# An encoder trunk on one Trainium2 core: another order of casts and sums at the begin of the MLP products

## The chip, the cores and the metric

The kernel runs on one core of a Trainium2 chip. The metric is device time in microseconds (us) of one execution; lower is better. Its engines are called as the profile calls them: PE (TensorE, matrix products; PEld is its weight load), DVE (VectorE), ACT (ScalarE), POOL (GpSimd) and SP (SyncE, which here issues most transfers; its own queue is SPq).

## What is computed

A trunk of two layers over 1024 frames with 1024 channels. Layer 0 mixes with RWKV-7 and gated DeltaNet heads, layer 1 with chunked softmax attention. Each layer then has the MLP on which the change works:

```python
for i in range(DEPTH):                      # DEPTH = 2
    h = rmsnorm(x, norm_mix_g[i])
    ...                                     # even: rwkv7_group and gdn_group, odd: chunk_band_attention
    x = x + mix                             # mix = heads @ w_out
    hf = rmsnorm(x, norm_ffn_g[i])
    x = x + jnp.square(jax.nn.relu(hf @ mlp_w1[i])) @ mlp_w2[i]
    x = x + rmsnorm(p[i] @ ple_w_proj[i], ple_norm_g[i]) * jax.nn.sigmoid(x @ ple_w_gate[i])
```

`mlp_w1` is 1024x4096 and `mlp_w2` 4096x1024; all is float32.

## The kernel before, in words

**Split products.** A float32 product is made of three matmuls on fp32r operands: each operand is cast to a high half (`hi`, on ACT), and the rest is its low half (`lo`, a subtraction on DVE). `mm3` multiplies hi by hi, hi by lo and lo by hi. So every operand that PE takes costs one pass of ACT and, behind it, one of DVE. `split` does both; `split_start` is the cast alone and `split_end` the subtraction alone.

**The MLP by sub-products.** Activations are held as channels by frames (128 partitions x 1024 frames), and a pair of channel tiles by two frame halves makes four blocks, `b11`, `b12` (even tile, first and second half of the frames), `b21`, `b22` (odd tile). The first product runs over 16 pairs p of hidden tiles; each pair needs seven sub-products instead of eight, in the order m = 1, 2, 5, 6, 7, 3, 4, each of 12 matmuls of 128x512. Their operands are blocks or differences of blocks: on the activations' side `cmb[m][j]` for four pairs j of channel tiles, on the weights' side what `prepare(p, m)` makes from `w1`. In the traces and the program's order the activations' operands are `r` (m = 1, 2, 7, 3), `xw`, `x` (5, 6) and `act` (4), and the weights' are `act` (the first `w`). A step, or slot, is k = 7p + q.

**Begin of the MLP.** `Trunk.tail` first makes eight output tiles n of the out-projection on the second half of the frames, 24 matmuls each; the first half came earlier. For each n: `load_x` brings the residual tile into `xr[n % 2]`; `first_half(n)` scales its first half by the norm's weight into `xs` (L1284) and, for odd n, casts `cmb[1]` and `cmb[2]` of the pair from it; then the projection; `ev_out(n)` evacuates it onto the residual (L1312), stores it, scales the second half, and for odd n below 7 makes `cmb[3]`, 5, 6, 7 and 4 (subtractions L1306, casts L1264, low halves L1268); `square` (L1289 and on) puts squares on ACT and sums them on POOL into `acc`. The norm's row factor is applied after the product. So the MLP can begin before it is known; `row_stats` sums `acc` over partitions by matmuls with `ones` (PE) behind slot 3, takes the mean on DVE (`ms`) and the inverse root on POOL, and `to_rows` turns it into rows `rs` behind slot 6 by transposes on PE (`ident`). POOL then scales hidden blocks by `rs`.

**What sets the order.** Up to and with the eight output tiles a scheduler places instructions by a time model, inside the limits of the data. From the line `self.pinned = True` on, each engine takes its instructions in the order in which the code emits them. The fourth pair's operands (n = 6 and 7) of products 5, 3, 6, 7 and 4 and the first pair's weights are made there, between the first seven products, by the list `ahead`: one entry per slot q of p = 0, carried out ahead of that slot's product.

**Handover to the second product.** It has 56 steps of 24 matmuls. Ahead of its first steps (p = 15), `load_hidden` splits hidden tiles that come back from memory, `load_block` fetches blocks of `w2`, `w_split` casts them and `w_sum` (POOL) adds or subtracts blocks. Blocks and splits are issued at slots q = 3, 5 and 4, 6 of p = 15.

Of the kernel before, what the change touches and what calls it, by code (L numbers as in the profile page):

```python
# [17 lines left out]
P = 128  # L18
# [97 lines left out]
class Trunk:  # L116
# [239 lines left out]
    def row_stats(self, accs, out, scale=1.0 / D, eps=1e-6, pool=False):  # L356

        nc = self.nc
        nt = out.shape[-1]
        ps = self.stat_bank()  # L360
        for i in range(nt):
            self.mm(ps[:, i:i + 1], accs[i // 4][:, (i % 4) * P:(i % 4 + 1) * P], self.ones[:, 0:1],
                             start=True, stop=True)
        ms = self.sm.tile([P, NT], F32, tag="ms", name="ms")[:, 0:nt]
# [829 lines left out]
    def tail(self, i, xsrc):  # L1194
# [13 lines left out]
        with ExitStack() as es:  # L1208
# [48 lines left out]
            sq = sq_pool.tile([P, HB], F32, tag="sq", name="sq")  # L1257
# [29 lines left out]
            def square(n, hf):  # L1287
# [4 lines left out]
                else:  # L1292
                    A.activation(sq, t, AF.Square)
                    G.tensor_tensor(accs[hf], accs[hf], sq, op=ALU.add)

            def first_half(n):
                scaled(n, 0)
                if n % 2:
                    j = n // 2
                    split(cmb[1][j], b11)  # L1300
                    split(cmb[2][j], b21)
                square(n, 0)

            def combine(m, j):
                u, v, w = {5: (b12, b12, b11), 6: (b22, b22, b12), 7: (b11, b22, b11), 4: (b21, b21, b22)}[m]
                V.tensor_tensor(u, v, w, op=ALU.subtract)  # L1306
                split(cmb[m][j], u)

            def ev_out(n):
                def f(ps):  # L1310
# [120 lines left out]
            def w_sum(g, m, n):  # L1431
# [4 lines left out]
                G.tensor_tensor(o, u, v, op=op)  # L1436

            def w_split(g, m, n):
# [28 lines left out]
            def ev_1(p, q, m, ps):  # L1467
                o = held[p]
                d = 8 if p == 0 else 7 * p + 2
# [36 lines left out]
            for p in range(16):  # L1506
# [6 lines left out]
                for q, m in enumerate(order):  # L1513
# [637 lines left out]
```

## Time and profile before

| | us |
|---|---|
| median of three runs | 3146.58 (3139.86 to 3149.94) |
| profiled execution | 3152.89 |
| its span, first to last instruction | 3151.1 |
| PE busy | 3020.8 (96%) |
| DVE busy | 2218.4 (70%) |
| ACT busy | 1410.3 (45%) |
| POOL busy | 1248.0 (40%) |
| mean granted clock of PE | 0.966 |

The profile is of one execution, 1.8 us longer than its span. A busy share over the whole span says little of a single place: PE can be full on average and wait in one stage. A timeline row gives the start and the busy time in us, the engine, the line of the kernel, the operation, out<-in, the shapes, how many instructions it holds (x), and in brackets the idle time of the engine just ahead of it with what ended it. A row of a stretch gives its length, the busy time and number of instructions of the engines named, then the granted clock of PE, the busy share of the DMA engines and GB/s. Layer 0's MLP begins at about 1016 us and hands over to its second product near 1350; layer 1's at about 2410 and 2750.

### The profile page before, as it was taken

To read this page: it belongs to the slowest core of one execution; us is meant where nothing else is said; L and a number is where in the kernel's file an instruction comes from. 1 tells how busy PE (TensorE), PEld (TensorE's weight loads), DVE (VectorE), ACT (ScalarE), POOL (GpSimd) and SP (SyncE) were. 2 spreads that over 40 slices of the span, in tenths; PEclk is the share of its full clock that TensorE was granted. 3 is DMA by queue.
4 is the path that set the end of the run, shared out by engine and by line. 5 is a ranking of instruction groups with operands and counts; after the bars stand their busy time and mean duration, and the time that the engine had idled before them with its cause. 6 is when DMAs were issued, how large, how long until landed. Compare 5 with 4: busy or idle time off the path is not lost.

```text
span 3151.1 us, 45431 instructions
## 1 busy us (share of the span) xinstructions
PE 3020.8 (96%) x17096; PEld 2525.7 (80%) x17096; DVE 2218.4 (70%) x3666; ACT 1410.3 (45%) x2464; POOL 1248.0 (40%) x1404
## 2 busy tenths in 40 slices
PE   7999999999998999999999999999998999999999
PEld 5887778788786788878888899998876888778887
DVE  6555774566847788878676587887867888777672
ACT  4343443343525454444334365665645454543341
POOL 6344342343612565557263200000113565656442
PEclk8999898999899999999999999999999999999999
DMA  3311112112234244574423211110154344664323
GB/s 115 102 60 60 44 32 77 60 60 83 103 126 144 100 151 149 179 257 168 143 87 132 95 36 43 41 49 27 65 181 167 117 147 151 221 220 168 133 89 105
DMA packets 160700, 353.60 MB, mean 112 GB/s; under 512 B 42592, under 2 KB 42720, under 8 KB 160480
## 3 DMA queue, kind: packets, MB, share of 16 engines
q1 hardware_dynamic: 128224, 291.97, 27.8%
q10 hardware_dynamic: 32256, 58.73, 4.9%
q8 instruction: 134, 2.20, 0.3%
q14 instruction: 86, 0.70, 0.1%
HBM read 251.02 MB, written 99.61 MB: 111 GB/s over the span
## 4 chain that ended last, share of the span: by engine, by line
PE 44%; DVE 6%; ACT 2%; issue 2%; DMA 1%; POOL 1%; SPq 0%; ACTq 0%; DVEq 0%; POOLq 0%
PE dps L173 40%; PE sc L173 2%; PE pt L178 1%; PE po L173 1%; DVE pb L2000 1%; POOL late L113 0%; DVE ptile L340 0%; PE dps L178 0%; DVE act L113 0%; DVE gw L1667 0%; ACT F L1942 0%; ACT pb L2004 0%; DVE r L1268 0%; DMA wraw<-in_w_out 0%; POOL act L113 0%
## 5 line engine op out<-in xcount | busy, mean ns | idle before, releaser
L173 PE MATMUL dps<-r,act 128*128 128x512 f32 x4440 | 1044.1, 394 | 21.5 <-ACT act L113 13.2
L173 PEld LDWEIGHTS dps<-r,act 128*128 128x128 f32 x4440 | 837.3, 189 | 214.1 <-ACT act L113 15.1
L173 PE MATMUL dps<-xg,whi 128*128 128x512 f32 x1280 | 439.1, 419 | 13.2 <-ACT xg L342 6.9
L113 ACT CAST act<-late 128x512 fp32r<-128x512 f32 (+1 forms) x282 | 200.8, 729 | 390.3 <-DVE late L113 213.6
L113 DVE TENSOR_TENSOR act<-late,act 128x512 fp32r<-128x512 f32 (+1 forms) x282 | 339.3, 1211 | 37.0 <-ACT act L113 31.0
L173 PE MATMUL dps<-wq,act 128*128 128x384 f32 x1536 | 305.4, 346 | 5.8 <-DVE vs L1909 2.1
L173 PEld LDWEIGHTS dps<-xg,whi 128*128 128x128 f32 x1280 | 248.3, 199 | 69.2 <-ACT xg L342 6.9
L173 PEld LDWEIGHTS dps<-wq,act 128*128 128x128 f32 x1536 | 266.1, 191 | 10.1 <-DVE vs L1909 3.3
L173 PE MATMUL dps<-xg,wlo 128*128 128x512 f32 x640 | 266.6, 417 | 2.1 <-DVE wlo L299 2.1
L113 POOL TENSOR_TENSOR late<-late 128x512 f32<-128x512 f32 (+1 forms) x104 | 179.9, 1733 | 106.8 <-ACT late L113 73.3
L113 POOL TENSOR_TENSOR late<-late,rs 128x512 f32<-128x512 f32 x88 | 133.9, 1528 | 86.3 <-DVE late L113 69.4
L1916 POOL TENSOR_TENSOR sq<-qk 128x512 f32<-128x512 f32 x32 | 34.7, 1083 | 311.4 <-ACT qk L1904 294.4
L113 DVE TENSOR_TENSOR r<-act,r 128x1024 fp32r<-128x1024 f32 (+1 forms) x80 | 148.4, 1859 | 5.5 <-ACT r L113 5.5
L173 PEld LDWEIGHTS dps<-xg,wlo 128*128 128x128 f32 x640 | 126.6, 198 | 29.1 <-DVE wlo L299 3.4
L173 PE MATMUL dps<-xw,act 128*128 128x512 f32 x576 | 139.2, 393 | 1.5 <-ACT act L113 1.5
L113 DVE TENSOR_TENSOR late<-late,dps 128x512 f32<-128x512 f32 x154 | 105.2, 683 | 44.6 <-PE dps L173 41.4
L298 ACT CAST whi<-wraw 128x1024 fp32r<-128x1024 f32 x78 | 81.6, 1046 | 119.2 <-PE dps L173 94.8
L173 PEld LDWEIGHTS dps<-xw,act 128*128 128x128 f32 x576 | 107.5, 188 | 28.2 <-ACT act L113 3.1
L2004 ACT ACTIVATE pb<-pb,mx 128x640 f32<-128x640 f32 (+4 forms) x128 | 89.6, 700 | 83.1 <-DVE mx L2002 79.5
L113 DVE TENSOR_TENSOR late<-late 128x512 f32<-128x512 f32 x120 | 123.8, 1032 | 1.0
L299 DVE TENSOR_TENSOR wlo<-wraw,whi 128x1024 fp32r<-128x1024 f32 x78 | 99.0, 1271 | 34.1 <-ACT whi L298 33.0
L113 ACT ACTIVATE late<-late 128x512 f32<-128x512 f32 x176 | 110.9, 631 | 25.7 <-POOL late L113 22.9
(490 smaller groups left out, 5865.7 us busy)
## 6 DMA issues: line engine op xcount, KB each, us to landing
late<-in_w SPq DMA_DIRECT2D x100, 512.0 KB
hc<-late ACTq DMA_DIRECT2D x154, 256.0 KB
act<-hc SPq DMA_DIRECT2D x76, 512.0 KB
wraw<-in_w_in SPq DMA_DIRECT2D x56, 512.0 KB
hraw<-hc SPq DMA_DIRECT2D x36, 512.0 KB
hc<-sums ACTq DMA_DIRECT2D x70, 256.0 KB
act<-in_w SPq DMA_DIRECT2D x28, 512.0 KB
wraw<-in_w_out SPq DMA_DIRECT2D x21, 512.0 KB
```

What stands on the lines that cost most here:

```text
L113: return lambda *args, **kw: self.tc.keep_in_program_order(f(*args, **kw))
L173: r = self.nc.tensor.matmul(out, lhsT, rhs, start=start, stop=stop)
L178: return self.nc.tensor.transpose(out, in_, ident)
L298: nc.scalar.copy(hi, raw)
L299: nc.vector.tensor_tensor(lo, raw, hi.bitcast(F32), op=ALU.subtract)
L1916: G.tensor_tensor(sq, q4[:, 8 * e:8 * e + 8], q4[:, 8 * e:8 * e + 8], op=ALU.mult)
L2000: V.tensor_tensor_reduce(S, ps[:, 0:n * P], toep[:, (5 - n) * P:], op0=ALU.add, op1=ALU.max, scale=1.0, scalar=NEG, accum_out=mx[:, 0:1])
L2004: A.activation(S, S, AF.Exp, bias=mx[:, 1:2], accum_out=l)
```

## The change

The change has seven parts, all in `tail` and the two functions that it calls for statistics.

- `row_stats` becomes `row_sums` (the matmuls with `ones`) and `row_norms` (mean and inverse root). At the MLP's begin the sums come behind slot 4 (was 3), the norms behind slot 5, `to_rows` behind slot 7 (was 6); the first pair's scaling moves from slot 8 to 9.
- `first_half(n)` casts `cmb[1]` or `cmb[2]` for every n, directly from the residual with the norm's weight as the scale (L1309 in the numbering after: scalar_tensor_tensor on DVE), where before both were cast for odd n from `xs`. It still fills `xs`.
- Two tiles `sq` in turn hold the squares, where there was one.
- `ev_out(n)` for odd n below 7 starts the operands of 5 and 3 together and then ends them; the square of tile 7's second half moves into the pinned part.
- `ahead` is written anew: sums and casts of the activations' operands (`x5`, `x3`, ...) and of the first pair's weights (`w2`, `w5`, ...) begin together and end later, in turn.
- `w_sum` of the first block row, m = 5, runs on VectorE instead of GpSimd.
- At p = 15 one hidden tile is split and one block fetched at each of q = 1 to 4, where two of each were at q = 3 and 5; the weight splits come at q = 3 and 5 instead of 4 and 6.

```diff
+        self.row_norms(self.row_sums(accs, out), out, scale, eps, pool)
...
-            sq = sq_pool.tile([P, HB], F32, tag="sq", name="sq")
+            sqs = ring([sq_pool.tile([P, HB], F32, tag=f"sq{q}", name="sq") for q in range(2)])
...
             def first_half(n):
+                c, t, g = cmb[1 + n % 2][n // 2], xr[n % 2][:, hs[0]], self.vec("ffng", 8 * i + n)
+                A.activation(c[:, 0], t, AF.Copy, scale=g)
+                V.scalar_tensor_tensor(c[:, 1], t, g, c[:, 0].bitcast(F32), op0=ALU.mult, op1=ALU.subtract)
                 scaled(n, 0)
-                if n % 2:
-                    j = n // 2
-                    split(cmb[1][j], b11)
-                    split(cmb[2][j], b21)
                 square(n, 0)
 
             def combine(m, j):
+                if m == 3:
+                    return split_start(cmb[3][j], b22)
                 u, v, w = {5: (b12, b12, b11), 6: (b22, b22, b12), 7: (b11, b22, b11), 4: (b21, b21, b22)}[m]
                 V.tensor_tensor(u, v, w, op=ALU.subtract)
-                split(cmb[m][j], u)
+                return split_start(cmb[m][j], u)
...
                     if n % 2 and n < 7:
-                        split(cmb[3][j], b22)
-                        for m in (5, 6, 7, 4):
-                            combine(m, j)
-                    square(n, 1)
+                        c5, c3 = combine(5, j), combine(3, j)
+                        split_end(*c5)
+                        split_end(*c3)
+                        for m in (6, 7, 4):
+                            split_end(*combine(m, j))
+                    if n < 7:
+                        square(n, 1)
...
-                G.tensor_tensor(o, u, v, op=op)
+                (V if (g, m) == (0, 5) else G).tensor_tensor(o, u, v, op=op)
...
-            ahead = [((prepare, 0, 2), (combine, 5, 3), (split, cmb[3][3], b22)), (), ((prepare, 0, 5),),
-                     ((combine, 6, 3), (prepare, 0, 6)), ((combine, 7, 3), (prepare, 0, 4), (prepare, 0, 7)),
-                     ((prepare, 0, 3),), ((combine, 4, 3),)]
+            begun = {}
+            def begin(*keys):
+                for key in keys:
+                    begun[key] = combine(int(key[1]), 3) if key[0] == "x" else part(0, int(key[1]))
+            def end(*keys):
+                for key in keys:
+                    split_end(*begun.pop(key))
+            ahead = [((begin, "w2", "x5", "x3", "w5"), (end, "w2", "x5")), ((end, "w5", "x3"), (begin, "x6", "w6")),
+                     ((end, "x6", "w6"), (begin, "x7", "w4"), (square, 7, 1)),
+                     ((end, "w4"), (begin, "w7"), (end, "x7"), (begin, "w3", "x4")), ((end, "w7", "w3", "x4"),), (), ()]
...
-                d = 8 if p == 0 else 7 * p + 2
+                d = 9 if p == 0 else 7 * p + 2
...
-                    if k == 3:
-                        self.row_stats(accs, col, pool=True)
-                    elif k == 6:
+                    if k == 4:
+                        stats = self.row_sums(accs, col)
+                    elif k == 5:
+                        self.row_norms(stats, col, pool=True)
+                    elif k == 7:
                         self.to_rows(col, rs)
                     if p == 15:
+                        if 1 <= q <= 4:
+                            load_hidden(q - 1)
+                            load_block(0, 2, q - 1)
                         if q in (3, 5):
-                            for r in (q - 3, q - 2):
-                                load_hidden(r)
-                                load_block(0, 2, r)
-                        if q in (4, 6):
-                            w_split(*steps[q // 2 - 2])
+                            w_split(*steps[q // 2 - 1])
```

Three places show what this does to the order of an engine's instructions. First DVE in layer 0, around the evacuation of output tile 7 (`act_10073` is the residual, `act_10074` is `xs`, `dps` a PSUM bank; `r_10054`, `r_10056` and `r_10058` hold operands of the products 1, 2 and 7). Before:

```order
L1306 TENSOR_TENSOR act_10074<-act_10074 128x512
L1268 TENSOR_TENSOR r_10058<-act_10074,r_10058 128x512
L1312 TENSOR_TENSOR act_10073<-act_10073,dps_10423 128x512
L1268 TENSOR_TENSOR act_10069<-act_10074,act_10069 128x512
L1268 TENSOR_TENSOR r_10054<-act_10074,r_10054 128x512
L1268 TENSOR_TENSOR r_10056<-act_10074,r_10056 128x512
L113 TENSOR_TENSOR act_10465<-act_10371,act_10465 128x512
L113 TENSOR_TENSOR act_10074<-act_10074 128x512
L113 TENSOR_TENSOR xw1_10065<-act_10074,xw1_10065 128x512
```

The same place after:

```order
L1309 SCALAR_TENSOR_TENSOR r_10054<-act_10073,vecs_60,r_10054 128x512
L1277 TENSOR_TENSOR x6_10066<-act_10074,x6_10066 128x512
L1309 SCALAR_TENSOR_TENSOR r_10056<-act_10073,vecs_60,r_10056 128x512
L1277 TENSOR_TENSOR r_10058<-act_10074,r_10058 128x512
L1323 TENSOR_TENSOR act_10073<-act_10073,dps_10424 128x512
L1277 TENSOR_TENSOR act_10069<-act_10074,act_10069 128x512
L113 TENSOR_TENSOR act_10074<-act_10074 128x512
L113 TENSOR_TENSOR act_10372<-act_10372 128x4x128
L113 TENSOR_TENSOR act_10464<-act_10372,act_10464 128x512
L113 TENSOR_TENSOR xw1_10065<-act_10074,xw1_10065 128x512
```

The two low halves into `r_10054` and `r_10056` stood behind the evacuation and now stand ahead of it. Behind it, sums (`act_10074`, `act_10372`) now come two at a time ahead of the subtractions that need their casts. From the evacuation to the low half of product 7's first weights, both counted, DVE has 22 rows before and 21 after; layer 1 has the same order.

Second, PE at the first seven products, as a difference (- before, + after; the second number of a shape counts columns, x the instructions).

```order
 L173 MATMUL dps<-x_10067,act 128x512 x3
+L173 MATMUL dps<-r,act 128x512 x12
 L173 MATMUL dps<-ones,acc 128x1 x8
-L173 MATMUL dps<-r,act 128x512 x24
-L173 MATMUL dps<-act 128x512 x9
+L173 MATMUL dps<-r,act 128x512 x12
+L173 MATMUL dps<-act 128x512 x12
+L173 MATMUL dps<-r,act 128x512 x12
 L178 MATMUL dps<-ident,col 128x128 x8
```

The product with `ones` moves from behind product 6 (its last rows are `x`) to behind product 7, and the transposes (`ident`) from inside product 4 to behind the next pair's product 1.

Third, DVE of layer 0 at the handover (`r` holds split hidden tiles, `act` split weights, `late` raw blocks, `xw` sums of the second product). Before:

```order
L113 TENSOR_TENSOR late<-late,dps 128x512
L113 TENSOR_TENSOR act<-late,act 128x1024 x2
L113 TENSOR_TENSOR r<-hraw,r 128x1024
L113 TENSOR_TENSOR xw_12850<-xw_12850,dps 128x512
L113 TENSOR_TENSOR act<-late,act 128x1024
L113 TENSOR_TENSOR r<-act,r 128x1024
```

After:

```order
L113 TENSOR_TENSOR late<-late,dps 128x512
L113 TENSOR_TENSOR act<-act,late 128x1024
L113 TENSOR_TENSOR act<-late,act 128x1024
L113 TENSOR_TENSOR r<-hraw,r 128x1024
L113 TENSOR_TENSOR xw_12851<-xw_12851,dps 128x512
L113 TENSOR_TENSOR act<-act,late 128x1024
L113 TENSOR_TENSOR act<-late,act 128x1024
L113 TENSOR_TENSOR r<-act,r 128x1024
```

The rows `act<-act,late` of 128x1024 are weight sums that were on POOL. Elsewhere, the scheduler's order of the attention stage of layer 1 (about 1700 to 2366 us) differs too, with the same instructions but those of the change.

More of the change, by code (lines that the diff above doesn't have):

```diff
@@ L356, in row_stats, with row_sums @@
     def row_stats(self, accs, out, scale=1.0 / D, eps=1e-6, pool=False):
-        nc = self.nc
+        self.row_norms(self.row_sums(accs, out), out, scale, eps, pool)
+    def row_sums(self, accs, out):
         nt = out.shape[-1]
@@ L363, in row_stats, with row_norms @@
                              start=True, stop=True)
+        return ps
+    def row_norms(self, ps, out, scale=1.0 / D, eps=1e-6, pool=False):
+        nc = self.nc
+        nt = out.shape[-1]
         ms = self.sm.tile([P, NT], F32, tag="ms", name="ms")[:, 0:nt]
@@ L1292, in square @@
                 else:
+                    sq = sqs()
                     A.activation(sq, t, AF.Square)
```

## The prediction

> **What bounds the kernel now.** I read the page first, for the whole span.
>
> ```profile
> span 3151.1 us, 45431 instructions
> ...
> PE 3020.8 (96%) x17096; PEld 2525.7 (80%) x17096; DVE 2218.4 (70%) x3666; ACT 1410.3 (45%) x2464; POOL 1248.0 (40%) x1404
> ...
> PE 44%; DVE 6%; ACT 2%; issue 2%; DMA 1%; POOL 1%; SPq 0%; ACTq 0%; DVEq 0%; POOLq 0%
> ```
>
> TensorE (PE) is busy 96% of the span and leads the chain that ended last. Only 130 us are idle, so an edit that leaves the matmuls as they are, as this one does, can win no more than idle time and time at a lowered clock. The next question is how much of both lies where the change works. The timeline of PE at the start of layer 0's first MLP product:
>
> ```profile
> 1006.03 10.82 PE L173 MATMUL dps<-xg,act 128*128 128x512 f32 x46 [3.44 <-DVE act L1268]
> 1016.69 2.20 PE L173 MATMUL dps<-r,w 128*128 128x512 f32 x9
> 1023.58 2.00 PE L173 MATMUL dps<-r,w 128*128 128x512 f32 x3 [4.68 <-ACT r L1264]
> 1027.24 1.22 PE L173 MATMUL dps<-r,act 128*128 128x512 f32 x2 [1.67 <-ACT act L113]
> ...
> 1036.43 1.91 PE L173 MATMUL dps<-xw,act 128*128 128x512 f32 x6 [0.67 <-ACT act L113]
> ...
> 1039.54 1.84 PE L173 MATMUL dps<-ones,acc 128*128 128x1 f32 x16
> 1045.63 7.19 PE L173 MATMUL dps<-r,act 128*128 128x512 f32 x24 [4.26 <-ACT act L113]
> ...
> 1054.73 1.03 PE L178 MATMUL dps<-ident,col 128*128 128x128 f32 x8
> ...
> 1061.80 4.29 PE L173 MATMUL dps<-xw,act 128*128 128x512 f32 x18
> ...
> 1067.29 5.67 PE L173 MATMUL dps<-r,act 128*128 128x512 f32 x24
> ```
>
> The rows with brackets are what to see: PE waits 4.68 us inside product 1 (`r,w`), 1.67 at product 2, 0.67 inside 6, and 4.26 ahead of product 7, each time for a cast of an operand that is made too late. The same place of layer 1:
>
> ```profile
> 2418.88 1.95 PE L173 MATMUL dps<-r,w 128*128 128x512 f32 x3 [5.98 <-ACT r L1264]
> 2423.93 1.22 PE L173 MATMUL dps<-r,act 128*128 128x512 f32 x2 [3.10 <-ACT act L113]
> ...
> 2442.29 8.49 PE L173 MATMUL dps<-r,act 128*128 128x512 f32 x24 [4.21 <-ACT act L113]
> ...
> 2459.79 4.29 PE L173 MATMUL dps<-xw,act 128*128 128x512 f32 x18
> ```
>
> The waits name ScalarE (ACT), so I asked for VectorE (DVE) by stretches: from the evacuation of out-projection tile 6 to that of tile 7 (layer 0, layer 1), and from there to the end of the low half of product 7's weights.
>
> ```profile
> 984.25:1021.05 36.80, 36.80 (x40) 1.00 0.53 186
> 2376.82:2416.87 40.05, 38.66 (x46) 1.00 0.49 168
> ```
> ```profile
> 1021.05:1046.33 25.28, 15.18 (x24) 0.71 0.25 93
> 2416.87:2442.96 26.09, 14.44 (x24) 0.77 0.24 90
> ```
>
> Up to tile 7's evacuation DVE has no idle time worth the name, so it sets when that comes. Behind it DVE is busy only 15.18 of 25.28 us: cast, subtraction, cast and subtraction stand in one chain on two engines, and each waits for the other. That chain is what the change rewrites. The idle time also costs clock, which the windows of 3 us show (third figure from the end):
>
> ```profile
> 1002.00:1005.00 3.00, 0.59 (x3) 0.16 (x1) 3.00 (x4) 3.00 (x6) 1.54 (x2) 1.00 0.30 100
> 1023.00:1026.00 3.00, 2.00 (x3) 0.79 (x3) 1.53 (x2) 2.17 (x5) 2.00 (x2) 0.50 0.92 328
> 1044.00:1047.00 3.00, 1.36 (x3) 1.09 (x4) 2.24 (x5) 0.62 (x1) 2.52 (x7) 0.50 0.00 0
> ```
>
> An idle stretch of 3.44 us left the clock at 1.00, one of 4.68 was followed by 0.50, and product 7 starts at 0.50 again: the 24 matmuls at 1045.63 take 7.19 us, and 24 at 1067.29 take 5.67. The Trainium skill (TensorE: Matmul & The Clock Gate, Part 1) has the clock halve after an idle window of about 3.4 us whose start runs freely; the two rows agree, and by it a remaining wait of 3 to 4 us could go either way (a rival below).
>
> **The change part by part.** *Begin of the first product* (the split from the residual, the interleaved sums and casts, the ones product later). Rows that price it:
>
> ```profile
> 1006.50 1.77 DVE L1268 TENSOR_TENSOR xw<-act,xw 128x512 fp32r<-128x512 f32 x1
> ...
> 1021.05 0.68 DVE L1312 TENSOR_TENSOR act<-act,dps 128x512 f32<-128x512 f32 x1
> 1021.65 0.68 DVE L1268 TENSOR_TENSOR act<-act 128x512 fp32r<-128x512 f32 x1
> ...
> 1045.61 0.72 DVE L113 TENSOR_TENSOR act<-act 128x512 fp32r<-128x512 f32 x1 [0.73 <-ACT act L113]
> ```
> ```profile
> 1005.98 1.74 POOL L1294 TENSOR_TENSOR acc<-acc,sq 128x512 f32<-128x512 f32 x1 [1.09 <-ACT sq L1293]
> ```
> ```profile
> L343 DVE SCALAR_TENSOR_TENSOR act<-xw,vecs,act 128x512 fp32r<-128x512 f32 x12 | 9.7, 810 | 9.5 <-ACT act L342 9.5
> ```
>
> Ahead of tile 7's evacuation DVE now has two more operations, the low halves of the fourth operands of products 1 and 2. A row costs 0.60 where nothing disturbs it (1021.05 to 1021.65), 0.81 as scalar_tensor_tensor, and 1.77 beside a sum of squares on GpSimd (POOL; its row overlaps); the mean of the stretch above is 36.80/40 = 0.92. I take 0.92: 2 x 0.92 = 1.8 us later, between 1.2 and 3.5. The Trainium skill (SBUF — State Buffer, Who interferes with whom) says that a VectorE instruction with two SBUF inputs and a reading GpSimd instruction block each other; the 1.77 beside 1.74 agrees, and by it alone the delay would be 3.5 and the whole sum below 3.4 us smaller.
>
> From the evacuation to the low half of product 7's weights stand 21 rows (22 before), but now each cast on ACT has another subtraction to hide behind. 21 x 0.61 = 12.8 us, one POOL sum beside them 1.1 (1.77 less 0.68), three visible casts at about 0.7 (the wait at 1045.61) 2.1: 16.0 us, where before took 25.28 and 26.09. With the 1.8 ahead the weights are whole 25.3 - 16.0 - 1.8 = 7.4 us sooner in layer 0 and 8.3 in layer 1, at 1038.9 and 2434.7. Without any visible cast it is 2 us less, with eight of them 3 more.
>
> From there PE has to do the rest of product 7 (10 of 12 matmuls, 2.3), the ones product (1.84, which filled a wait before and now stands exposed), products 3 and 4 and the next pair's 1 and 2 (4 x 2.75, a half of 5.5 for 24), and the transposes (0.8): 15.9 us. Before, the next pair's product 5 began at 1061.80 and 2459.79; now at 1054.8 and 2450.6. That is 7.0 and 9.2 us, together **14.5 with a margin**: 16.2 by this sum, less 1.7 for one layer that falls to half clock once more. With every unknown bad it is 3, with every one good 21.
>
> *The statistics' chain* follows the ones product on POOL and must end ahead of the transposes:
>
> ```profile
> 1041.68 0.57 POOL L274 TENSOR_SCALAR col<-ms 128x8 int32<-128x8 int32 x1 [13.64 <-DVE ms L365]
> ...
> 1047.69 0.52 POOL L279 TENSOR_TENSOR col<-col,rsw 128x8 f32<-128x8 f32 x1
> ```
>
> It takes 6.5 us. Three products of 2.75 now stand between, 8.25; the mean's row waits on DVE behind eight others, some 1.5 us. So it is just hidden; if not, 1 us per layer. The scaling of p = 0 a slot later costs nothing, since its results are read back a hundred slots on. A second tile of squares lets ACT run ahead of POOL in the DVE-bound stretch, where ACT has room: nothing.
>
> *Handover to the second product* (a block's weight sums on VectorE, the hidden loads and splits one per slot). In both layers:
>
> ```profile
> 1343.00:1378.00 35.00, 31.11 (x129) 23.28 (x128) 28.13 (x21) 17.60 (x21) 26.16 (x11) 1.00 0.84 297
> 2741.00:2776.00 35.00, 30.93 (x129) 23.30 (x128) 27.83 (x21) 17.60 (x22) 26.15 (x11) 1.00 0.84 294
> ```
> ```profile
> 1367.76 5.80 POOL L113 TENSOR_TENSOR act<-act,late 128x1024 f32<-128x1024 f32 x2
> ```
> ```profile
> 1375.15 1.21 DVE L113 TENSOR_TENSOR act<-act 128x1024 fp32r<-128x1024 f32 x1
> ```
> ```profile
> 1377.56 17.68 PE L173 MATMUL dps<-r,act 128*128 128x512 f32 x76 [1.22 <-DVE r L113]
> ```
>
> ```profile
> PE dps L173 <- DVE r L113: 2.1, 3, 1.2
> PE dps L173 <- DVE act L113: 1.8, 3, 1.0
> ```
>
> PE idles 3.89 and 4.07 us of 35, in layer 0 in six waits (the last fence, PE's waits between 1343 and 1380) of which the last is the 1.22; that is all there is to win. POOL is busy 26.16 us, and its sums take 2.9 us each (5.80/2); on DVE, which is busy 28.13, they cost 1.21 each, 4.8 for four. That takes DVE to 33 of 35, so the wait is cut and not ended. I take 2.5 a layer: **5**, between 0 and 8.
>
> *Attention of layer 1.* The scheduler orders the same instructions another way there.
>
> ```profile
> 1770.00:2260.00 490.00, 466.25 (x3046) 445.45 (x3045) 384.89 (x1003) 285.96 (x632) 37.39 (x57) 1.00 0.12 41
> ```
>
> PE idles 23.75 of 490 us. Nothing in the change aims at it, and the order gives no sign: 0, with 6 either way.
>
> **The sum:** -14.5 - 5 + 0 = -19.5 us. The profiled execution took 3152.89 (1.8 outside its span), so it would take 3133.4; the median of the three runs, 3146.58, lies 6.3 lower, and on its scale the forecast is 3127.
>
> **The rivals.** *A: the clock stays low.* If DVE's extra rows meet POOL's sums (3.5 instead of 1.8) and the casts show in full, the wait ahead of product 7 stays above some 4 us and both layers keep the 0.50. For it speaks that 4.26 was enough before; against it that the first wait of 4.68 falls away, as product 1 no longer needs anything behind tile 7's evacuation. The begin then wins 6, the sum is -11: 3136. *B: the sums on VectorE only move the handover's wait.* DVE at 94% of that stretch, and two-input operations that block against POOL's scaling, delay the low halves that PE waits for. For it: all six PE waits there name DVE. The handover gives 0: 3132. POOL loses 11.6 us of its work in the same stretch, so there is less to meet, and I give it little. By the Trainium skill (SBUF — State Buffer, Who interferes with whom) it is the likelier way, since the sums read SBUF twice; the 1.77 agrees with the rule, and no row of before shows it for operations of 1024 columns. *C, slower: attention's new order.* If a cast or copy there moves behind a longer one, PE's idle time grows. It decides the sign when it costs over 28.9 us (19.5 and the 9.4 of the bound below), so the 23.75 would have to more than double: 3157. Against it: the instructions are the same and DVE is busy 385 of 490, not full. *D: attention takes back part,* 10 to 28 us: 3137 to 3155.
>
> **How the numbers follow.** A measurement of this kernel tells 0.3%, 9.4 us, from no change. Forecast 0.60, A 0.12 (half of it within the bound), B 0.09, C 0.07, D 0.12. Faster: 0.60 + 0.09 + 0.06 = 0.75; same: 0.12 + 0.06 = 0.18; slower 0.07. The range reaches from 3115 (begin 19, handover 8, attention 4.5 the good way) to 3141, which holds A, B and the lower half of D.
>
> **What would show it.** Right: no PE wait over 2 us inside the first product 1 in either layer; the low half of product 7's weights some 16 us behind tile 7's evacuation and the next pair's product 5 some 32 us behind it (40.8 and 42.9 before); PE idle under 2.5 us in the 35 us around the handover, with no 128x1024 sum on POOL at its begin. Wrong: tile 7's evacuation over 4 us later, a PE wait over 4 us ahead of product 7 with a clock of 0.50, handover waits unchanged, or an attention stage longer than before by over 10 us.

## The result, and the profile after

The changed kernel takes 3129.38 us, the median of five runs (3121.61 to 3140.74), against 3147.0 (3139.86 to 3150.07) for the kernel before: a ratio of 0.9944, with a 95% interval of 0.9916 to 0.9972. The profiled execution is the longest of the five, 3140.74 us, 12.1 under the profiled execution of before. Its page:

```profile
span 3139.0 us, 45439 instructions
...
PE 3024.9 (96%) x17096; PEld 2534.6 (81%) x17096; DVE 2227.6 (71%) x3674; ACT 1409.8 (45%) x2464; POOL 1225.8 (39%) x1396
```

The begin of layer 0's first product, in the timeline of PE:

```profile
987.31 23.74 PE L173 MATMUL dps<-xg,act 128*128 128x512 f32 x94 [2.08 <-DVE act L1277]
...
1014.19 6.95 PE L173 MATMUL dps<-xg,act 128*128 128x512 f32 x22 [3.14 <-DVE act L1277]
1020.98 2.90 PE L173 MATMUL dps<-r,w 128*128 128x512 f32 x12
1026.09 0.73 PE L173 MATMUL dps<-r,act 128*128 128x512 f32 x2 [2.21 <-ACT act L113]
...
1037.22 0.73 PE L173 MATMUL dps<-r,act 128*128 128x512 f32 x2 [1.99 <-ACT act L113]
1040.18 4.64 PE L173 MATMUL dps<-r,act 128*128 128x512 f32 x10 [2.23 <-DVE act L113]
1044.62 3.41 PE L173 MATMUL dps<-ones,acc 128*128 128x1 f32 x16
1047.88 5.42 PE L173 MATMUL dps<-r,act 128*128 128x512 f32 x12
...
1062.25 4.29 PE L173 MATMUL dps<-xw,act 128*128 128x512 f32 x18
```

The wait of 4.68 us inside product 1 is gone: its twelve matmuls run through. The wait ahead of product 7 is still there, in two pieces (1.99 and 2.23) with 0.73 us of work between them. New is what follows it: ten matmuls take 4.64 us, the ones product 3.41 (1.84 before) and product 3 takes 5.42 where twelve matmuls take 2.9. And the out-projection has waits of 2.08 and 3.14, and a short one of 0.53, where it had one of 3.44. So the next pair's product 5 begins at 1062.25, and at 1061.80 before. Layer 1:

```profile
2410.24 2.90 PE L173 MATMUL dps<-r,w 128*128 128x512 f32 x12
2416.72 0.73 PE L173 MATMUL dps<-r,act 128*128 128x512 f32 x2 [3.58 <-ACT act L113]
...
2430.81 3.55 PE L173 MATMUL dps<-r,act 128*128 128x512 f32 x10 [2.22 <-DVE act L113]
2434.15 3.41 PE L173 MATMUL dps<-ones,acc 128*128 128x1 f32 x16
2437.42 5.28 PE L173 MATMUL dps<-r,act 128*128 128x512 f32 x12
...
2451.66 4.29 PE L173 MATMUL dps<-xw,act 128*128 128x512 f32 x18
```

On DVE, the evacuation of tile 7 in both layers, and the row that holds the low half of product 7's weights in layer 0 (the first of three):

```profile
1024.08 0.67 DVE L1323 TENSOR_TENSOR act<-act,dps 128x512 f32<-128x512 f32 x1
...
1039.45 1.88 DVE L113 TENSOR_TENSOR act<-act 128x512 fp32r<-128x512 f32 x3
```
```profile
2414.71 0.67 DVE L1323 TENSOR_TENSOR late<-late,dps 128x512 f32<-128x512 f32 x1
```

From the evacuation to the matmuls that take the low half: 1040.18 - 1024.08 = 16.1 us and 2430.81 - 2414.71 = 16.1. The handovers, 35 us each from the same matmul on as in the rows of before, and the stretch of attention:

```profile
1343.45:1378.45 35.00, 33.99 (x146) 26.92 (x145) 32.89 (x31) 17.64 (x21) 12.73 (x7) 1.00 0.97 350
2732.87:2767.87 35.00, 33.97 (x147) 27.04 (x146) 32.86 (x31) 17.62 (x21) 12.71 (x7) 1.00 0.98 346
1766.70:2256.70 490.00, 468.04 (x3032) 447.58 (x3031) 381.20 (x993) 284.69 (x629) 38.46 (x57) 0.99 0.12 39
```

PE idles 1.0 us at each handover instead of 3.9 and 4.1, DVE is busy 32.9 us of 35, POOL 12.7 instead of 26.2. In attention PE idles 22.0 of 490 us (23.75 before).

**Where the 12.1 us come from,** by the times at which the same matmul begins in both traces. "Out-projection" is, in layer 0, from the first matmul with the weights fetched ahead to product 1, in layer 1 the last four tiles; "seven products" is from there to the next pair's product 5.

| stage | before | after | difference |
|---|---|---|---|
| all ahead of layer 0's out-projection | 972.36 | 970.44 | -1.9 |
| out-projection, layer 0 | 37.42 | 43.43 | +6.0 |
| seven products, layer 0 | 45.11 | 41.28 | -3.8 |
| handover, layer 0 | 65.41 | 61.65 | -3.8 |
| on to layer 1's last four output tiles | 985.74 | 984.23 | -1.5 |
| out-projection, layer 1 | 23.19 | 27.60 | +4.4 |
| seven products, layer 1 | 49.14 | 41.42 | -7.7 |
| handover, layer 1 | 76.91 | 72.94 | -4.0 |

The two long middles of the first product take the same time to 0.01 us (274.50 and 276.80), and the rest behind the second handover to 0.02. On PE the first row holds the same instructions in the same order, so I count its 1.9 as no effect of the change. In this execution the begin (both out-projections and both seven products) gives 1.1 us in all, and the handover 7.7.

The longer out-projections are only in part waits. PE idles 5.74 us in layer 0's instead of 3.44, and 3.13 instead of 0.28 in layer 1's; the rest, 3.7 and 1.6 us, is the same matmuls at a lower clock (mean granted clock of the stage 0.92 instead of 0.98, and 0.94 instead of 1.00).

### The profile page after: what moved, and what is told of

It is laid out like the page before. It is cut to its first block, busy times and chain, and to the rows that moved or that the text cites. A ratio compares the mean times of both kernels' runs of the same rounds, so it can differ in the third digit from the quotient of the medians.

```text
span 3139.0 us, 45439 instructions
## 1 busy us (share of the span) xinstructions
PE 3024.9 (96%) x17096; PEld 2534.6 (81%) x17096; DVE 2227.6 (71%) x3674; ACT 1409.8 (45%) x2464; POOL 1225.8 (39%) x1396
## 5 line engine op out<-in xcount | busy, mean ns | idle before, releaser
L173 PE MATMUL dps<-xg,whi 128*128 128x512 f32 x1280 | 436.7, 417 | 12.6 <-ACT xg L342 7.1
L1939 POOL TENSOR_TENSOR sq<-qk 128x512 f32<-128x512 f32 x32 | 35.7, 1116 | 318.2 <-ACT qk L1927 293.3
L113 DVE TENSOR_TENSOR r<-act,r 128x1024 fp32r<-128x1024 f32 (+1 forms) x80 | 137.8, 1722 | 6.7 <-ACT r L113 6.7
```

What stands on the lines that cost most here:

```text
L113: return lambda *args, **kw: self.tc.keep_in_program_order(f(*args, **kw))
L173: r = self.nc.tensor.matmul(out, lhsT, rhs, start=start, stop=stop)
L1939: G.tensor_tensor(sq, q4[:, 8 * e:8 * e + 8], q4[:, 8 * e:8 * e + 8], op=ALU.mult)
```

## The experiments

The stages of the table, for all kernels (us, from the PE timelines; matmuls added ahead of product 7 or 2 lie inside the seven products). Each row of stages is one profile, the ratio is of all runs of that kernel. Where nothing of layer 0's out-projection was changed, it is 37.4 us in before and 39.0 in three kernels, and layer 1's with one square tile and the new split is 23.8 to 26.0, so a stage that differs by under about 2 us is not told apart from no change. By the ratios no variant of the changed kernel is told apart from it; the experiments speak by the stages.

| kernel | out-proj. 0 | seven 0 | out-proj. 1 | seven 1 | begin, difference to before | ratio to before (95%) |
|---|---|---|---|---|---|---|
| before | 37.4 | 45.1 | 23.2 | 49.1 | 0 | 1 |
| changed | 43.4 | 41.3 | 27.6 | 41.4 | -1.1 | 0.9944 (0.9916 to 0.9972) |
| changed, again | 44.0 | 40.2 | 28.0 | 41.4 | -1.2 | 0.9945 (0.9927 to 0.9962) |
| handover alone | 39.0 | 44.7 | 23.0 | 48.2 | 0.0 | 0.9972 (0.9961 to 0.9984) |
| its sums alone | 39.0 | 44.7 | 23.0 | 48.3 | +0.1 | one run |
| one square tile | 39.4 | 37.9 | 25.0 | 39.2 | -13.4 | 0.9933 (0.9919 to 0.9946) |
| unpinned part as before | 37.4 | 39.3 | 22.9 | 45.9 | -9.4 | 0.9930 (0.9917 to 0.9943) |
| split from the scaled copy | 37.7 | 44.0 | 27.4 | 37.4 | -8.3 | 0.9934 (0.9919 to 0.9948) |
| ones product early | 44.7 | 34.2 | 27.2 | 37.8 | -11.0 | 0.9944 (0.9925 to 0.9962) |
| wait filled | 43.4 | 35.4 | 27.4 | 35.7 | -13.0 | 0.9928 (0.9911 to 0.9945) |
| before, wait filled | 39.0 | 43.0 | 23.1 | 47.2 | -2.6 | 0.9991 (0.9980 to 1.0003) |
| one tile, wait filled | 40.8 | 36.4 | 26.0 | 39.2 | -12.6 | 0.9933 (0.9918 to 0.9949) |
| one tile, two waits filled | 40.8 | 36.4 | 23.8 | 39.3 | -14.7 | 0.9919 (0.9899 to 0.9939) |
| one tile, old operand order, wait filled | 40.7 | 36.3 | 25.2 | 39.2 | -13.4 | 0.9928 (0.9910 to 0.9946) |

**The changed kernel again.** No edit.

> The changed kernel once more, unchanged, for how much of its profile repeats. The trace of the changed kernel shows the out-projection of layer 0 (from its first matmul with the weights fetched ahead to the first matmul of product 1) at 43.4 us instead of 37.4, the first seven products from there to the next pair's product 5 at 41.3 instead of 45.1 (layer 0) and 41.4 instead of 49.1 (layer 1), and some 3.8 us less at each handover. Theory 1 (waits set these stages): the same stages come out within 1.5 us of these values, the median is 3129 with 5 either way, and runs differ by the granted clock alone. Theory 2 (the profile caught a bad execution, the begin wins 14 us elsewhere): the stages differ by over 4 us between the two profiles.

The stages of the begin repeat within 1.1 us, the median is 3131.09. So the waits of the begin are no accident of one profile. Both profiled executions (3140.74 and 3141.72) lie some 10 us over their medians, at a mean granted clock of 0.965 and 0.966; the three runs of this kernel at 0.972 took 3121.61 to 3125.84. Runs of one kernel differ by the clock.

**The handover alone,** and of it the sums alone (the first two lines), in the kernel before.

```diff
-                G.tensor_tensor(o, u, v, op=op)
+                (V if (g, m) == (0, 5) else G).tensor_tensor(o, u, v, op=op)
...
+                        if 1 <= q <= 4:
+                            load_hidden(q - 1)
+                            load_block(0, 2, q - 1)
                         if q in (3, 5):
-                            for r in (q - 3, q - 2):
-                                load_hidden(r)
-                                load_block(0, 2, r)
-                        if q in (4, 6):
-                            w_split(*steps[q // 2 - 2])
+                            w_split(*steps[q // 2 - 1])
```

> The kernel before with only the two handover edits (a block row's sums on VectorE, one hidden tile and one block per slot). Theory 1: the PE idle time of the 35 us around each handover falls from about 4 to under 0.5 us, 7.5 us in all, nothing else changes by over 1 us except by the clock, and the time is 7.5 us under before (ratio 0.9976). Theory 2 (the handover was hidden, or its gain needs the changed begin): no change of the time, and the waits at the handover stay or come back within the first steps of the second product.

> The kernel before with the first block row's sums on VectorE and nothing else, one profile. Theory 1 (PE waits there for sums on GpSimd, 2.9 us each behind one another): the PE idle time around the handover falls by 2.5 to 4 us in each layer, so these sums alone are nearly all of the handover's gain. Theory 2 (the pairs of hidden tiles and blocks at one slot hold VectorE up, and GpSimd is not waited for): it stays at 3.9 and 4.1, or grows by up to 2, since VectorE has 4.8 us more to do.

The sums alone, the windows of the two handovers from the same matmul on:

```profile
1341.98:1376.98 35.00, 32.64 (x137) 24.98 (x136) 30.95 (x27) 19.54 (x23) 13.64 (x7) 1.00 0.93 326
2735.56:2770.56 35.00, 33.77 (x145) 26.55 (x144) 32.92 (x30) 19.70 (x23) 14.03 (x7) 1.00 0.95 338
```

PE idles 2.4 and 1.2 us, 1.5 and 2.8 less than before (2.5 to 4 were expected, which layer 0 misses). With both edits it idles 2.2 and 1.0, where under 0.5 was expected. Against the stages of the first table the sums alone win 1.96 and 3.70, both edits together 1.95 and 4.03: the sums are the gain, and one hidden tile and block per slot adds nothing in layer 0 and 0.3 in layer 1. The 7.5 expected for both edits was too much: 6.0 by these stages. Layer 0 wins 3.3 to 4.5 us only in the kernels with the new begin; why the rest needs it is not settled. In time the handover alone is 0.28% faster.

**One tile for the squares,** in the changed kernel.

```diff
-            sqs = ring([sq_pool.tile([P, HB], F32, tag=f"sq{q}", name="sq") for q in range(2)])
+            sqs = ring([sq_pool.tile([P, HB], F32, tag=f"sq{q}", name="sq") for q in range(1)])
```

> The changed kernel with one tile for the squares, as before. With one tile the scheduler puts the low half of output tile 3's weights ahead of tile 2's evacuation on VectorE again. Theory 1 (the longer out-projection of layer 0 comes from that order: the low half stands behind an evacuation that waits for a residual tile's transfer): layer 0's out-projection falls from 43.4 us to about 40, layer 1's stays, and the time is about 3 us under that of the changed kernel. Theory 2 (it comes from the two extra operations per pair on a VectorE without idle time, the split from the residual): layer 0's out-projection stays within 1 us of 43.4.

Layer 0's out-projection falls to 39.4, as theory 1 has it; layer 1's falls by 2.7, which neither foresaw. In the trace of the changed kernel the flipped order shows on DVE: tile 2's evacuation waits for the residual's transfer, and the low half of tile 3's weights (128x1024) stands behind it, which PE waits for (2.08 above).

```profile
985.43 0.69 DVE L1323 TENSOR_TENSOR act<-act,dps 128x512 f32<-128x512 f32 x1 [1.74 <-DMA act<-in_x]
986.03 3.44 DVE L1277 TENSOR_TENSOR act<-act 128x1024 fp32r<-128x1024 f32 x2
```

With one tile the low half comes first:

```profile
980.96 1.23 DVE L1277 TENSOR_TENSOR act<-act 128x1024 fp32r<-128x1024 f32 x1 [0.98 <-ACT act L1273]
983.20 0.69 DVE L1323 TENSOR_TENSOR act<-act,dps 128x512 f32<-128x512 f32 x1 [1.01 <-DMA act<-in_x]
```

The begin wins 12.3 us more than in the changed kernel, and only 6.7 of them are out-projection. The other 5.6 are the seven products: here the clock does not fall at the wait ahead of product 7, though that wait is still there. PE in layer 0:

```profile
1036.26 2.58 PE L173 MATMUL dps<-r,act 128*128 128x512 f32 x10 [1.79 <-DVE act L113]
1038.67 1.84 PE L173 MATMUL dps<-ones,acc 128*128 128x1 f32 x16
1040.37 3.01 PE L173 MATMUL dps<-r,act 128*128 128x512 f32 x12
...
1052.38 4.29 PE L173 MATMUL dps<-xw,act 128*128 128x512 f32 x18
```

From the low half to the next pair's product 5 it is 16.1 us in both layers (22.1 and 20.9 in the changed kernel). No edit touches that place, so this part of the 12.3 cannot be put down to the tile itself.

**The unpinned part as before, and the split from the scaled copy.** The first undoes the split from the residual, the second tile and the new operand order; the second the split alone. The split's edit in the changed kernel:

```diff
             def first_half(n):
-                c, t, g = cmb[1 + n % 2][n // 2], xr[n % 2][:, hs[0]], self.vec("ffng", 8 * i + n)
-                A.activation(c[:, 0], t, AF.Copy, scale=g)
-                V.scalar_tensor_tensor(c[:, 1], t, g, c[:, 0].bitcast(F32), op0=ALU.mult, op1=ALU.subtract)
                 scaled(n, 0)
+                if n % 2:
+                    j = n // 2
+                    split(cmb[1][j], b11)
+                    split(cmb[2][j], b21)
```

> The changed kernel with the unpinned part as before: one tile of squares, products 1 and 2 cast from the scaled copy after odd tiles, operands 3, 5, 6, 7, 4 made one after another. Kept are the interleaved pinned sums and casts, the later ones product and the handover. Theory 1 (the out-projection loses 6 and 4 us to the edits ahead of the pinned part, the pinned part wins by itself): both out-projections are back at before's length within 1 us, product 1 waits again over 2 us for the fourth operand of product 1, the seven products still take 2 to 5 us less than before in each layer, and the time is within 4 us of the changed kernel, either way. Theory 2 (the split from the residual is what wins): the seven products take as long as before within 1 us, and the time is that of the handover edits alone.

> The changed kernel with products 1 and 2 cast from the scaled copy for odd tiles, as before; two tiles of squares and the new order of the other operands stay. Theory 1 (the split from the residual is what the out-projection pays for and what ends the wait inside product 1): both out-projections fall back to within 1 us of before (37.4 in layer 0), product 1 waits again by over 3 us, and from the begin of product 1 to the next pair's product 5 it takes 3 to 6 us less than before in layer 0. Theory 2 (the second tile of squares makes the out-projection longer): layer 0's out-projection stays over 41 us.

With all three undone both out-projections are as before (37.4, 22.9), product 1 waits again, and the begin still wins 9.4 us: theory 1 (the seven products take 5.8 and 3.2 us less than before, where 2 to 5 were expected). PE in layer 0:

```profile
1013.70 2.20 PE L173 MATMUL dps<-r,w 128*128 128x512 f32 x9
1021.09 0.79 PE L173 MATMUL dps<-r,w 128*128 128x512 f32 x1 [5.19 <-ACT r L1273]
...
1036.83 2.58 PE L173 MATMUL dps<-r,act 128*128 128x512 f32 x10 [1.78 <-DVE act L113]
...
1052.96 4.29 PE L173 MATMUL dps<-xw,act 128*128 128x512 f32 x18
```

With the split alone undone layer 0's out-projection is back (37.7), layer 1's is not (27.4): theory 1 for layer 0, against it for layer 1. Product 1 waits again, 5.2 us in layer 0; but layer 0's seven products take only 1.1 us less than before, where 3 to 6 were expected, as the clock falls at product 7 there (20.9 us from the low half on, 16.1 in layer 1). By these profiles the split costs layer 0 about six us with two tiles and two with one; in layer 1 the second tile costs 2.7 with the split and 4.5 without, and the split with one tile 2. The six and the 4.5 are clear of the spread that stands above the table, the twos are not. Why the second tile costs layer 1 anything was not looked into.

**The ones product early,** in the changed kernel (with the scaling from slot 8 again).

```diff
-                    if k == 4:
-                        stats = self.row_sums(accs, col)
-                    elif k == 5:
-                        self.row_norms(stats, col, pool=True)
-                    elif k == 7:
+                    if k == 3:
+                        self.row_stats(accs, col, pool=True)
+                    elif k == 6:
                         self.to_rows(col, rs)
```

> The changed kernel with the statistics' matmuls, norms and rows at the slots of before (3 and 6) and the first pair's scaling at slot 8 again. Theory 1 (the ones product fills the wait ahead of product 7 for nothing and behind product 7 costs its own time): the ones product takes 1.8 us in the wait, the stretch from product 7's low half to the next pair's product 5 falls by 1.8 to 3.4 us, more where the clock then stays up, and the time is 2 to 8 us under that of the changed kernel. Theory 2 (moving it later is what lets VectorE run on, since the mean's row waits for PE in the middle of the chain): the low half of product 7's weights comes 3 us later, as the mean's wait of 3.1 us stands ahead of it again, and the time is 1 to 3 us over that of the changed kernel.

The seven products take 7.1 and 3.6 us less than in the changed kernel, and the low half of product 7's weights comes no later behind the evacuation (16.2 us in layer 0, 1029.66 to 1045.83); so theory 1 by the trace. The gain is more than the 1.84 at which the sum had the ones product, because the clock is at 0.50 for only 3.41 us behind the wait in each layer (13.66 and 10.24 in the changed kernel). The rows of layer 0:

```profile
1040.69 1.96 PE L173 MATMUL dps<-ones,acc 128*128 128x1 f32 x16
...
1045.83 6.75 PE L173 MATMUL dps<-r,act 128*128 128x512 f32 x22 [2.29 <-DVE act L113]
```

The time, 3133.9 (3121.1 to 3136.77), shows no gain and so does not bear the expected 2 to 8 us out.

**The wait filled,** in the changed kernel's `product`.

```diff
+                if (p, m) == (0, 7):
+                    for _ in range(10):
+                        self.mm(ps, prep[0][1][1][:, 0, 0:P], cmb[1][0][:, 0], start=True, stop=True)
```

> The changed kernel with ten matmuls of 128x512 more in front of product 7 of the first pair, into the bank that product 7 then starts afresh; they are ready at once, take 2.3 us and lie inside the wait for the low half of product 7's weights. In both profiles of the changed kernel the clock falls to half behind that wait for 10 to 14 us, and from that low half to the next pair's product 5 PE takes 22.1 and 20.9 us (layers 0 and 1) where 15.9 was forecast. Theory 1 (the wait, 4.2 us with 0.7 of work in it, lowers the clock, and that is where the begin's gain went): with the wait filled the clock stays at 1.00, the 22.1 and 20.9 become 16 to 17, and the time is 5 to 10 us under that of the changed kernel though PE does more. Theory 2 (the half clock comes from elsewhere, the ones product and the rest are slow in themselves): the stretch stays within 1 us, and the time is the same or 1 to 2 us longer.

PE of the filled kernel, layer 0, with the added matmuls (`r,w`), and layer 1's two ends:

```profile
1032.73 2.48 PE L173 MATMUL dps<-r,w 128*128 128x512 f32 x10
1035.04 0.63 PE L173 MATMUL dps<-r,act 128*128 128x512 f32 x2
1037.83 2.57 PE L173 MATMUL dps<-r,act 128*128 128x512 f32 x10 [2.16 <-DVE act L113]
1040.24 1.84 PE L173 MATMUL dps<-ones,acc 128*128 128x1 f32 x16
1041.94 3.01 PE L173 MATMUL dps<-r,act 128*128 128x512 f32 x12
...
1053.95 4.29 PE L173 MATMUL dps<-xw,act 128*128 128x512 f32 x18
```
```profile
2420.37 2.57 PE L173 MATMUL dps<-r,act 128*128 128x512 f32 x10 [2.13 <-DVE act L113]
...
2436.46 4.29 PE L173 MATMUL dps<-xw,act 128*128 128x512 f32 x18
```

The ones product takes 1.84 again and product 3 takes 3.01; from the low half to the next pair's product 5 it is 16.1 us in both layers (22.1 and 20.9 in the changed kernel). The clock in the changed kernel (PE alone), and in the filled one (all engines):

```profile
1033.00:1036.00 3.00, 2.23 (x10) 1.00 0.00 0
1036.00:1039.00 3.00, 0.73 (x2) 1.00 0.00 0
1039.00:1042.00 3.00, 1.82 (x4) 0.58 0.00 0
1042.00:1045.00 3.00, 3.00 (x10) 0.50 0.00 0
```
```profile
1034.00:1038.00 4.00, 1.84 (x9) 1.17 (x8) 4.00 (x8) 2.29 (x4) 0.00 (x0) 1.00 0.00 0
1038.00:1042.00 4.00, 4.00 (x27) 3.57 (x27) 3.27 (x6) 0.62 (x1) 0.00 (x0) 1.00 0.02 4
```

That is theory 1: 20 matmuls more, and the begin wins 13.0 us instead of 1.1. All kernels together say the same. From the low half on it is 16.1 us in seven of the eight stretches of the four changed kernels with a filled wait (in the eighth no wait is left), and the clock stays at 1.00 in all eight. In those without a fill that keep the ones product behind product 7 it is 16.1 in four stretches and 20.9 to 22.1 in six, and in these six the clock fell. So the unfilled wait lowers the clock in some executions and not in others, and the fill takes that chance away. The time, 3125.66, is 4 to 5 us under the changed kernel's two medians; the ratios' intervals overlap, so in time this step is not shown.

**Before, filled.** The same edit in the kernel before.

> The kernel before with the ten matmuls of 128x512 in front of product 7. Theory 1 (a wait with little work in it lowers the clock, in before too, where product 7 starts at 0.50 after 4.26 us): from product 7's start to the next pair's product 5 PE takes 16 us where it took 16.2 and 17.5, so the fill alone wins 1 to 2 us a layer less what it adds, and the time is that of before within 3 us: the fill wins much only where the change has put the ones product and three products right behind the wait. Theory 2 (the filled matmuls win by themselves, whatever stands behind): the time is 5 us or more under before.

From product 7 on it takes 15.6 us in both layers, against 16.2 and 17.5, and the time is that of before: theory 1. So in the traces the fill pays only where the change has put work right behind the wait.

**Three combinations:** one tile of squares and the filled wait; also product 2's wait filled (`if p == 0 and m in (2, 7)`); and the first with the odd tiles' operands in the old order.

> The changed kernel with one tile of squares and the filled wait ahead of product 7. Theory 1 (the two edits act on different places): layer 0's out-projection near 39.4 us, the low half of product 7's weights to the next pair's product 5 in 16.1 us in both layers, and a time at or a little under that of the filled kernel (3126 there), about 0.7 to 0.8% under before. Theory 2 (one tile won its 4 us only by the phase of the clock): the out-projection is back over 41 us and the time is over 3126.

> As the kernel with one tile of squares and a filled wait, with ten more matmuls in front of product 2, where PE waits 5.8 us in layer 0 (1.84 and 3.97) and 6.0 in layer 1 and the clock falls to half for 7 us. Theory 1 (the wait's length is set by VectorE and ScalarE, so filling it delays nothing and keeps the clock): no half clock between product 2 and product 5, 1 to 2 us less per layer, since most of the 7 us at half clock are idle anyway. Theory 2 (this wait is hidden behind the later one for product 7): the clock stays at 1.00 and the stage is no shorter, as product 7's low half comes no sooner.

> As the kernel with one tile of squares and a filled wait, with the operands of odd tiles made one after another again (3, 5, 6, 7, 4) ahead of the pinned part. Theory 1 (VectorE is full there, so starting 5 and 3 together wins nothing): the out-projections and the time within 2 us of the kernel with one tile of squares and a filled wait. Theory 2 (the new order lets VectorE run on and shortens that stretch): the out-projection of one layer at least is 2 us longer than there.

The first has 16.1 us behind the low half in both layers, as theory 1 says, but an out-projection of 40.8, between the two theories, and at 3129.62 its time is no better than the 3125.66 of the fill alone, which is theory 2's side. Filling product 2's wait too keeps the clock at 1.00 from product 2 to 5 in layer 0 and leaves the seven products at 36.4 and 39.3 (36.4 and 39.2 without): theory 2, that wait is hidden behind the later one. The old operand order changes neither out-projection by over 1 us, as theory 1 says. Its time is 3126.0, 3.6 under the first's where 2 was the most expected, but the intervals of the two ratios overlap. That of the two filled waits is 3126.69. Both are below the changed kernel's median, and no interval separates them from it.

## Why the prediction was right, and where it was not

The forecast, 3127, is 2 us from the median. Its sum did not come about in the way it was written, in the two executions of the changed kernel that have a trace: the begin, forecast at 14.5, won 1.1 and 1.2 there, and the handover 7.7 and 8.1 instead of 5. If the handover's 7.7 holds in the median execution, its begin wins some 10 us (an estimate, 17.6 less 7.7). So a begin that came out too small and a handover that came out larger made up for each other, and that the time is met to 2 us is in part luck.

- *From the evacuation to the low half of product 7's weights:* right. Forecast 16.0, measured 16.1 in both layers.
- *Tile 7's evacuation later by 1.8, between 1.2 and 3.5:* mis-sized. From the stage's start it comes at 46.5 us instead of 41.8 in layer 0 (+4.8) and at 32.1 instead of 29.4 in layer 1 (+2.7). I counted the two operations that pass the evacuation of tile 7, and not the out-projection tiles ahead of it: there the split from the residual and the second tile of squares ("nothing" in the prediction) put rows ahead of low halves that PE waits for, and the matmuls behind these waits ran at a lower clock. Undone together, both stages are as before. How much each takes differs between the layers.
- *15.9 us from there to the next pair's product 5, with half clock in one layer once:* the step that failed. It was 22.1 and 20.9. The term was right at full clock, 16.1 with the wait filled. The clock fell in both layers, for the whole of the ones product and of product 3 or nearly so, which the change puts right behind the wait. In before more of the time at half clock was waiting: 7.7 of 17.1 us in layer 0's seven products and 5.6 of 17.1 in layer 1's; in the changed kernel it is 0.7 of 13.7 and none of 13.7. That is rival A's mechanism, whose price (6 us won at the begin) was still too mild for these two executions: 1.1 and 1.2 won.
- *The ones product costs 1.84 where it stands now:* 3.41 in these executions, 1.84 where the wait is filled. Put back into the wait it holds up nothing in the trace: the low half of product 7's weights comes no later.
- *The signs named ahead:* no wait inside product 1, as forecast; product 5 of the next pair came 38.2 and 37.0 us behind the evacuation, where 32 was named as right (40.8 and 42.9 before), and tile 7's evacuation in layer 0 came over 4 us later, which was named as wrong.
- *Handover 5, between 0 and 8:* it won 7.7. The wait was for the sums on POOL, and DVE was busy 32.9 us of 35, the 33 forecast, and PE idles 1.0: rival B did not come. The other half of the edit does nothing measurable. One reading for B was wrong: the trace of before does hold a slow VectorE row of 1024 columns beside a POOL sum, 1.99 us at 987.20 against 1.23 at 984.25.
- *Attention 0:* right, 1.5 us in this pair of profiles, less than a stage of unchanged instructions differs by (all ahead of layer 0's out-projection, -1.9 us in the first profile of the changed kernel and +3.1 in the second). Rivals C and D did not come.

What stays open: the medians differ by 17.6 us, the profiled executions by 12.1. Both profiles of the changed kernel come from executions with a low clock. That others lose less of it at the begin would fit the medians. No trace of the changed kernel shows such an execution, but two things in the traces speak for it: related kernels with the same unfilled wait kept their clock in four stretches of six, which is worth five to six us each; and the two long stages outside begin and handover (rows one and five of the first table) take 1954.7 and 1955.9 us in the two profiles of the changed kernel, where the mean of all fourteen is 1954.8, so these executions are not long on their account.

## What to carry to other kernels

When a wait on the bounding engine is cut, look at what the change puts right behind the wait that remains: at a lowered clock that work cost nearly double here (5.42 us instead of 2.90 for twelve matmuls), and ten added matmuls in the wait bought it back in the trace, though no gain in time was shown. Cost an edit in a scheduled region by the order it gives to every row ahead of the point that counts, above all the second operands that the bounding engine takes; an additional buffer can flip it. And compare traces stage by stage at the same matmul, with a second profile of each kernel: two opposite changes of 5 us each show there, and the total hides them.

## What the runs showed of the hardware

- The clock fell behind a stretch that was not idle: 0.73 us of work in the 3 us from 1036 and two waits of 1.99 and 2.23, each shorter than the 3.44 that left it at 1.00 in before. Nor does the length of a wait decide: the same wait of 3.44 us in the same place was followed by 0.50 in the handover kernel (from 1002.10 to 1005.51), and the 46 matmuls behind it took 12.39 us instead of 10.82. In the changed kernel it then stayed at 0.50 past 1052 although PE was full from 1042 on (the rows below, of the changed kernel). The Trainium skill (TensorE: Matmul & The Clock Gate, Part 1) speaks of an idle window; here little work in a window was enough, and the measurement decides.

```profile
1048.00:1052.00 4.00, 4.00 (x11) 3.13 (x11) 3.34 (x6) 0.00 (x0) 3.02 (x9) 0.50 0.00 0
1052.00:1056.00 4.00, 4.00 (x17) 3.25 (x16) 0.69 (x1) 0.00 (x0) 0.90 (x5) 0.86 0.00 0
```

- In all fourteen traces a stretch at half clock lasts 3.41 us or a whole multiple of it (13.66 in the one above), the last record of a trace apart.
- One kernel's time moves with the granted clock of the run: 3121.61 us at 0.972 and 3140.74 at 0.965, with the same instructions. That is more than most edits here are worth.
- The middle of the first product, without a wait and at a clock of 1.00, takes 274.48 to 274.50 us in layer 0 and 276.78 to 276.80 in layer 1 in all fourteen profiles; the difference between executions lies in stages with waits.
